# Who forms the low halves of the weights: GpSimd and VectorE, or VectorE alone

## The chip, the cores and the metric

The kernel runs on one core of one Trainium2 chip. The metric is the device time of one execution in microseconds (us).

## The reference

Four layers work on 256 context tokens and 256 latent tokens of 1024 channels. Layers 0 and 3 mix by a gated linear recurrence (HGRN2, 8 heads of 128), layer 1 by attention over a window and the context (16 heads of 64), layer 2 by a state-space scan (S5). Behind every mixer comes a feed-forward network (FFN) with a three-tap convolution. The part that matters here is the dense products:

```python
def conv_ffn(h, w_in, conv_w, conv_b, w_out):
    u = dwconv_centred(h @ w_in, conv_w, conv_b)
    a, v = jnp.split(u, 2, axis=-1)
    return (jax.nn.silu(a) * v) @ w_out

def hgrn2_mixer(h_ctx, h_lat, w_in, lower, out_g, w_out):
    ...
        q, i, g, zf, zb = jnp.split(h @ w_in, 5, axis=-1)
    ...
            f = lb + (1.0 - lb) * jax.nn.sigmoid(p[gate_idx])
            ...
            o, s = gla_chunk_scan(flip(p[0]), flip(1.0 - f), flip(p[1]), flip(logf), s0)
```

All inputs are float32. The last layer's output for the latent tokens is returned.

## The kernel before

Each dense product is made of three matmuls with operands of a shorter format (fp32r): activations and weights are each split into a high half (the value rounded to the short format) and a low half (the rest), and TensorE sums high by high, high by low, and low by high (`mm3`, L691 to L693; `vproj`, L727 to L729).

The weights come as a stream of 248 tiles of [128, up to 2048] float32 (class `Stream`). `_load` (L96) issues one DMA on SP's queue into `wraw` (two buffers). `_split` (L103) takes the next tile and puts a list of small jobs into `todo`: the two high halves `whi` on ScalarE (L112), the low halves `wlo = wraw - whi` (L115), and the load of the tile two further on. `step` (L128) emits one job of the list. `mm3` and `vproj` call it after every second k, that is after every six matmuls, so that the split of the next tile is spread over the products with the present one: eight steps for two projections of eight k. What is left over is emitted when the next tile is fetched (`get`, L141), or in a burst in a layer's `chain` (L511). No scheduler moves instructions: each engine runs its own in the order in which the program emits them.

The low half is formed in two parts, side by side: GpSimd (POOL in the profile) takes the first `share` of the columns, VectorE (DVE) the rest. `SH` (L68) holds the shares: 0.5, and 0.65 in the HGRN layers. `run` and `chain` set the share (L1829, L498, L554); the FFN of layer 3 runs with the HGRN share too, since the last `chain` ahead of it sets that one.

In an HGRN layer, while TensorE makes the projections of head h+1, a generator `attn` (L1054) works on head h, one round at each `tick` (L700): TensorE's small products of the block (L1106), then VectorE multiplies `FB` by the gates (`double`, L1077 and L1082), multiplies the gates `P` by each other (L1088) and copies the block into `S` (L1111). The next round's products need the new `FB`. The gate of the projection just made is applied on VectorE between the rounds (`gate`, L1047).

At the end of a stage `chain` (L495) makes the norm: a reciprocal on VectorE (L465), then the update of `x` and the next input `h`, with some of the elementwise work on GpSimd (L520, L581). TensorE has little else to do meanwhile. While layers 0 and 1 run their FFN, constants of the S5 layer are made (`s5_prep`, L1462: `W` on VectorE, L1483 to L1488, `Wt` on GpSimd, L1482).

Of the kernel before, what the change touches and what calls it, by code (L numbers as in the profile page):

```python
# [6 lines left out]
F32 = mybir.dt.float32  # L7
# [57 lines left out]
NN = 18  # L65
PC = 18
PN = 12
SH = (0.5, 0.5, 0.65, 0.5, 0.5)  # L68
RNG = ((0, 256), (256, 512))
EPS = 1e-6  # L70
MUL, ADD, SUB, MAX = ALU.mult, ALU.add, ALU.subtract, ALU.max
# [10 lines left out]
class Stream:  # L82
    def __init__(self, kern, bufs, lead, hl_bufs):
        self.k = kern
        self.plan = []
        self.bufs, self.lead, self.hl = bufs, lead, hl_bufs
        self.nl = self.ns = self.nu = 0
        self.raw, self.split = {}, {}
        self.share = SH[0]
        self.todo = []  # L90
        self.cap = 1 << 20

# [10 lines left out]
    def _split(self):  # L103
        k, nc = self.k, self.k.nc
        key, ap, n = self.plan[self.ns]
        r = self.raw.pop(self.ns)
        hi = k.wp.tile([128, 2048], F32R, name="whi", bufs=self.hl)
        lo = k.wp.tile([128, 2048], F32R, name="wlo", bufs=self.hl)
        m = int(n * self.share) // 64 * 64

        def high(a, b):
            nc.scalar.activation(hi[:, a:b], r[:, a:b], AF.Copy)  # L112

        def low(e, a, b):
            e.tensor_tensor(lo[:, a:b], r[:, a:b], hi[:, a:b].bitcast(F32), op=SUB)  # L115

        if m:
            self.todo += [(high, 0, m), (low, nc.gpsimd, 0, m)]
        if m < n:
            self.todo += [(high, m, n), (low, nc.vector, m, n)]  # L120
        if m and m < n:
            self.todo[-3:-1] = self.todo[-2:-4:-1]
        if self.nl < min(len(self.plan), self.cap):
            self.todo.append((self._load,))
        self.split[self.ns] = (hi, lo)
        self.ns += 1
# [28 lines left out]
class Kern:  # L155
# [32 lines left out]
        h = self.xp.tile([128, 2, 2, NK, 256], F32R, name="h")  # L188
        self.hh, self.hl = h[:, 0], h[:, 1]

# [1 line left out]
    def tick(self):  # L192
        if not self.gens:
            self.bgtick()
        if not self.draining:
            for g in list(self.soft):
                self.advance(g, self.soft)
        gens = list(self.gens)
        if self.pace and len(gens) > 1:
            self.turn += 1  # L200
            if self.turn % self.pace:
                gens = [gens[(self.turn - 1) % len(gens)]]
        for g in gens:
            self.advance(g, self.gens)
# [45 lines left out]
            except StopIteration:  # L250
                self.bg = None

# [1 line left out]
    def consts(self):  # L254
        nc, cp = self.nc, self.cp
        self.cc = cp.tile([128, 16], F32, name="cc")
        nc.sync.dma_start(self.cc, self.a["cc"])
        self.x = self.xp.tile([128, NK, T], F32, name="x")
        for k in range(NK):
            (nc.scalar if k % 2 else nc.sync).dma_start(self.x[:, k], self.a["xin"][:, k])  # L260
        self.sel = cp.tile([128, 2], F32, name="sel")
        nc.sync.dma_start(self.sel, self.a["sel"])
        self.ident = cp.tile([128, 128], F32, name="ident")
        nc.sync.dma_start(self.ident, self.a["ident"])
        self.vec = cp.tile([128, NVEC], F32, name="vec")
        nc.sync.dma_start(self.vec, self.a["vec"])
        self.y = self.xp.tile([128, 2, NK, 256], F32, name="y")
        self.new_h()
        self.ones = cp.tile([128, 1], F32, name="ones")
        nc.vector.memset(self.ones, 1.0)  # L270
        self.epsc = cp.tile([128, 1], F32, name="epsc")
        nc.vector.memset(self.epsc, EPS)
        self.mT = cp.tile([128, 4, 6, NK, 2], F32, name="mT")
        self.g1 = cp.tile([128, 4, 4, NK, 2], F32, name="g1")
        self.sT = cp.tile([128, NK, 32], F32, name="sT")
        nc.vector.memset(self.sT, 0.0)
        nc.scalar.activation(self.sT[:, :, 0:2], self.cc.rearrange("p (k i) -> p k i", i=2), AF.Silu)

# [1 line left out]
    def mod_setup(self, pool, bufs, first, n):  # L280
        self.mod_pool, self.MB = pool, bufs
        self.mod_nl = self.mod_nd = first
        self.mod_end = n
        self.mod_raw = {}
        self.mod_pend = None
        self.mod_order = [(0, s, b) for b in range(4) for s in (1, 0)]
        self.mod_order += [(l, s, b) for l in range(4) for s in (1, 0, 2, 4, 3, 5) for b in range(4) if l or s > 1]
        for i in range(bufs):
            if first == 0 and i == 2:
                self.ws.start()  # L290
            self.mod_load()
# [124 lines left out]
        if self.mod_pend is not None and self.mod_pend[0] <= idx:  # L416
            self.mod_flush()

# [1 line left out]
    def rstd_col(self, sqs, nb, n):  # L420
        nc = self.nc
        ps = self.aux()
        for b in range(nb):
            for i, q in enumerate(sqs):
                nc.tensor.matmul(ps[:, b:b + 1], q[:, b * 128:(b + 1) * 128], self.ones, start=(b == 0 and i == 0),
                                 stop=(b == nb - 1 and i == len(sqs) - 1), skip_group_check=True)
        r = self.np_.tile([128, 8], F32, name="rs", bufs=4)
        nc.scalar.activation(r[:, :nb], ps[:, :nb], AF.Sqrt, scale=1.0 / n, bias=self.epsc)
        nc.vector.reciprocal(r[:, 4:4 + nb], r[:, :nb])
        return r  # L430
# [64 lines left out]
    def chain(self, l, n, half, nxt):  # L495
        nc = self.nc
        a, b = RNG[half]
        self.ws.share = SH[1]  # L498
        if n is not None:
            for _ in range(CW[0] if half else C0 if n == 1 else CS[2] if nxt is not None and KINDS[nxt[0]] == 2 else C3):  # L500
                yield
# [49 lines left out]
            return  # L551
        yield
        _, bc = yield from self.rstd_sb(("x", half))
        self.ws.share = SH[self.shi]  # L554
        l2, n2 = nxt
        s0 = 0 if n2 == 0 else 3
        s5 = n2 == 0 and KINDS[l2] == 2
# [2 lines left out]
        for k in range(NK):  # L560
            g = self.g1[:, l2, n2, k, half:half + 1]
            m = self.mT[:, l2, s0, k, half:half + 1]
# [12 lines left out]
            else:  # L575
                hi, lo = self.hh[:, half, k], self.hl[:, half, k]
# [97 lines left out]
            while ws.todo:  # L674
                ws.step()

# [1 line left out]
    def H(self, k, half):  # L678
        if half is None:
            return self.hh[:, :, k, :], self.hl[:, :, k, :]  # L680
        return self.hh[:, half, k, :], self.hl[:, half, k, :]
# [158 lines left out]
            self.nc.scalar.activation(y, ps, AF.Copy)  # L840
        return done

# [1 line left out]
    def plan_ffn(self, l, halves):  # L844
        tail = FTAIL if l < 3 and KINDS[l + 1] == 2 else 0
        add = self.ws.add
# [143 lines left out]
            while self.bg is not None:  # L990
                self.bgtick()

# [1 line left out]
    def lower_prep(self):  # L994
        nc = self.nc
        lg = self.v("low").rearrange("p (l k) -> p l k", k=NK)
# [234 lines left out]
            if full:  # L1231
                self.finish(c0)

# [1 line left out]
    def plan_na(self, l):  # L1235
        for _ in self.plan_heads(l, ("qk",), (lambda j: self.a["b_qk"][j], lambda p: self.a["b_v"][p]), 1):
            self.plan_wo(l, 0, 2)
        for _ in range(2):
            self.plan_wo(l, 1, 2)
            self.plan_wo(l, 2, 2)  # L1240
# [128 lines left out]
                    c0 = c  # L1369
            self.finish(c0)  # L1370

# [1 line left out]
    def cmul(self, e, outr, outi, ar, ai, br, bi, t):  # L1373
        e.tensor_tensor(outr, ar, br, op=MUL)
        e.tensor_tensor(t, ai, bi, op=MUL)
        e.tensor_tensor(outr, outr, t, op=SUB)
        e.tensor_tensor(outi, ar, bi, op=MUL)
        e.tensor_tensor(t, ai, br, op=MUL)
        e.tensor_tensor(outi, outi, t, op=ADD)
# [436 lines left out]
    def run(self):  # L1816
        nc, tc = self.nc, self.tc
        for l in range(4):
            (self.plan_hgrn, self.plan_na, self.plan_s5, lambda l: None)[KINDS[l]](l)
            self.plan_ffn(l, (1,) if l == 3 else (0, 1))  # L1820
        self.consts()
        with tc.tile_pool(name="start", bufs=1) as sp:
            self.mod_setup(sp, 7, 0, 8)
            self.begin()
        self.mod_setup(self.wp, 1, 8, 96)
        for l in range(4):
            halves = (1,) if l == 3 else (0, 1)
            self.shi = (2, 3, 0)[KINDS[l]] if KINDS[l] < 3 else 0
            self.ws.share = SH[self.shi]  # L1829
            if KINDS[l] == 3:  # L1830
                self.drain()
                self.mod_until(l, 3)
                for half in halves:
                    for k in range(NK):
                        hi, lo = self.H(k, half)
                        y = self.y[:, half, k]
                        nc.vector.tensor_tensor(y, hi.bitcast(F32), lo.bitcast(F32), op=ADD)
                        self.sq_add(("y", half), k, y)
                    self.gens.append(self.chain(l, 1, half, (l, 2)))
                    self.drain()  # L1840
            else:
                (self.hgrn, self.na, self.s5)[KINDS[l]](l)
            if l == 3:
                self.drain()
            self.shi = 0 if l < 3 else 4
            self.ffn(l, halves, (l + 1, 0) if l < 3 else None)
        self.drain()
# [85 lines left out]
```

## Time and profile before

| | |
|---|---|
| time, median of 3 runs (lowest to highest) | 2995.45 us (2994.34 to 2996.59) |
| the profiled execution: its span, the only time listed for it | 3001.2 us |
| TensorE (PE) busy | 2769.3 us, 92% |
| VectorE (DVE) busy | 2016.9 us, 67% |
| ScalarE (ACT) busy | 1285.0 us, 43% |
| GpSimd (POOL) busy | 824.1 us, 27% |
| L115 on GpSimd, 248 instructions | 627.8 us, mean 2532 ns |
| L115 on VectorE, 248 instructions | 400.5 us, mean 1615 ns |
| granted TensorE clock, mean | 0.960 |

Busy times overlap between engines. Only work or waiting on the engine that is late adds to the time. PE is TensorE's matmul row. An idle time in front of an instruction is put down to the semaphore that came last. A granted clock of 1.00 is 2.4 GHz, 0.50 is 1.2 GHz.

### The profile page before, as it was taken

The numbers are of one execution on the slowest core, as the hardware profiler recorded it, in microseconds if no ns is written. First come the engines' busy times: TensorE is split into PE (matmuls) and PEld (weight loads), VectorE is DVE, ScalarE is ACT, GpSimd is POOL, SyncE is SP. The second block draws the span as 40 slices with busy tenths as digits, with TensorE's granted clock in tenths as the row PEclk, the third lists the DMA queues.
The fourth block names the chain that finished last, engine by engine and source line by source line (L and its number), as shares of the span: only waits on it lengthen the run. The fifth ranks groups of instructions, "written<-read, shape, count | busy, mean of one in ns | idle before, by whom it ended". The sixth has DMA issues, their size and how long they took to land.

```text
span 3001.2 us, 53651 instructions
## 1 busy us (share of the span) xinstructions
PE 2769.3 (92%) x21814; PEld 2283.6 (76%) x21814; DVE 2016.9 (67%) x3979; ACT 1285.0 (43%) x2154; POOL 824.1 (27%) x440
## 2 busy tenths in 40 slices
PE   8999997999999999889999876989999888998998
PEld 5777776877788777777778734878888887776998
DVE  5676767776657555687555675378677777776776
ACT  4333333633344544553333565453333453332644
POOL 1111112243324111234332311332221342222443
PEclk9999998999999999999999988999999989998998
DMA  6222321255424342235553388323433442232543
GB/s 248 91 100 85 114 86 71 94 186 187 160 105 144 113 162 106 102 128 192 198 197 140 129 238 255 139 87 139 147 133 138 153 171 102 99 113 89 186 173 116
DMA packets 127046, 421.28 MB, mean 140 GB/s; under 512 B 36048, under 2 KB 55760, under 8 KB 102096
## 3 DMA queue, kind: packets, MB, share of 16 engines
q1 hardware_dynamic: 118608, 391.64, 37.5%
q0 software_dynamic: 5472, 23.07, 2.2%
q8 instruction: 172, 2.82, 0.4%
q10 hardware_dynamic: 2720, 3.15, 0.3%
q14 instruction: 74, 0.61, 0.1%
HBM read 392.78 MB, written 29.23 MB: 141 GB/s over the span
## 4 chain that ended last, share of the span: by engine, by line
PE 65%; DVE 20%; ACT 6%; issue 4%; DMA 3%; SPq 1%; POOL 1%; DVEq 0%; ACTq 0%; POOLq 0%
PE acc L691 16%; PE acc L692 15%; PE acc L693 15%; DVE wlo L115 3%; ACT whi L112 2%; PE aux L317 2%; PE aux L1106 2%; DVE FB L1077 2%; PE acc L727 1%; PE acc L729 1%; PE acc L728 1%; DVE y L564 1%; DVE u L896 1%; DVE P L1047 1%; PE aux L1146 1%
## 5 line engine op out<-in xcount | busy, mean ns | idle before, releaser
L115 POOL TENSOR_TENSOR wlo<-wraw,whi 128x1024 fp32r<-128x1024 f32 (+5 forms) x248 | 627.8, 2532 | 1738.2 <-ACT whi L112 1634.2
L691 PE MATMUL acc<-h,whi 128*128 128x512 f32 (+1 forms) x2368 | 869.7, 367 | 26.8 <-ACT h L577 15.7
L692 PE MATMUL acc<-h,whi 128*128 128x512 f32 (+1 forms) x2368 | 843.2, 356 | 21.1 <-DVE h L584 16.7
L693 PE MATMUL acc<-h,wlo 128*128 128x512 f32 (+1 forms) x2368 | 838.8, 354 | 6.1 <-POOL wlo L115 4.0
L691 PEld LDWEIGHTS acc<-h,whi 128*128 128x128 f32 x2368 | 459.1, 194 | 96.5 <-ACT h L577 18.8
L115 DVE TENSOR_TENSOR wlo<-wraw,whi 128x1024 fp32r<-128x1024 f32 (+5 forms) x248 | 400.5, 1615 | 184.5 <-ACT whi L112 154.5
L692 PEld LDWEIGHTS acc<-h,whi 128*128 128x128 f32 x2368 | 459.7, 194 | 81.4 <-DVE h L584 24.0
L693 PEld LDWEIGHTS acc<-h,wlo 128*128 128x128 f32 x2368 | 459.6, 194 | 67.0 <-POOL wlo L115 4.6
L112 ACT ACTIVATE whi<-wraw 128x1024 fp32r<-128x1024 f32 (+5 forms) x496 | 479.5, 1014 | 68.5 <-PE acc L692 51.2
L691 PE MATMUL acc<-gh,whi 128*128 128x256 f32 (+1 forms) x872 | 297.7, 341 | 11.2 <-ACT gh L897 11.2
L693 PE MATMUL acc<-gh,wlo 128*128 128x256 f32 (+1 forms) x872 | 289.6, 332 | 3.0 <-POOL wlo L115 3.0
L692 PE MATMUL acc<-gl,whi 128*128 128x256 f32 (+1 forms) x872 | 289.7, 332 | 1.0 <-DVE gl L898 0.7
L886 ACT ACTIVATE u<-acc,vec 128x512 f32<-128x512 f32 (+1 forms) x190 | 127.4, 691 | 215.1 <-PE acc L693 214.6
L1077 DVE TENSOR_TENSOR FB<-FB,P 128x256 f32<-128x256 f32 x384 | 165.4, 473 | 37.9 <-PE aux L1106 35.2
L691 PEld LDWEIGHTS acc<-gh,whi 128*128 128x128 f32 x872 | 167.5, 192 | 28.8 <-ACT gh L897 12.0
L889 DVE SCALAR_TENSOR_TENSOR u<-acc,vec,u 128x510 f32<-128x510 f32 (+1 forms) x190 | 122.0, 642 | 97.6 <-ACT u L886 97.5
L693 PEld LDWEIGHTS acc<-gh,wlo 128*128 128x128 f32 x872 | 167.0, 192 | 19.9 <-POOL wlo L115 3.8
L692 PEld LDWEIGHTS acc<-gl,whi 128*128 128x128 f32 x872 | 167.2, 192 | 17.7 <-DVE gl L898 2.3
L896 DVE TENSOR_TENSOR u<-u,u 128x512 f32<-128x512 f32 (+1 forms) x95 | 107.5, 1131 | 37.5 <-ACT u L895 34.2
L897 ACT ACTIVATE gh<-u 128x512 fp32r<-128x512 f32 (+1 forms) x95 | 52.3, 551 | 179.6 <-DVE u L896 179.6
L890 DVE SCALAR_TENSOR_TENSOR u<-acc,vec,u 128x510 f32<-128x510 f32 (+1 forms) x190 | 123.1, 648 | 6.7
L1106 PEld LDWEIGHTS aux<-FB 128*32 128x32 f32 (+1 forms) x4416 | 58.4, 114 | 82.0 <-DVE FB L1077 37.4
(299 smaller groups left out, 4328.4 us busy)
## 6 DMA issues: line engine op xcount, KB each, us to landing
wm<-in_w_mod SPq DMA_DIRECT2D x192, 512.0 KB, 5.0
wraw<-in_f_w_in SPq DMA_DIRECT2D x89, 1024.0 KB, 4.8
wraw<-in_fo SPq DMA_DIRECT2D x44, 896.0 KB, 4.5
wraw<-in_a_qz SPq DMA_DIRECT2D x18, 1024.0 KB, 4.9
wraw<-in_a_zg SPq DMA_DIRECT2D x18, 1024.0 KB, 4.9
wraw<-in_fo SPq DMA_DIRECT2D x16, 1024.0 KB, 4.9
wraw<-in_a_v SPq DMA_DIRECT2D x15, 1024.0 KB, 4.9
wraw<-in_c_glu SPq DMA_DIRECT2D x12, 1024.0 KB, 4.8
```

Source lines behind the costliest of these rows:

```text
L112: nc.scalar.activation(hi[:, a:b], r[:, a:b], AF.Copy)
L115: e.tensor_tensor(lo[:, a:b], r[:, a:b], hi[:, a:b].bitcast(F32), op=SUB)
L317: nc.tensor.matmul(ps[32 * j:32 * j + 32, :256], self.sT[:, k, :], r[q][:, j, :], start=(q == 0), stop=(q == 1), tile_position=(0, 32 * j))
L691: nc.tensor.matmul(ps, wh[:, k], hh, start=(first and k == 0), stop=False, **kw)
L692: nc.tensor.matmul(ps, wh[:, k], hl, start=False, stop=False, **kw)
L693: nc.tensor.matmul(ps, wl[:, k], hh, start=False, stop=(last and k == nk - 1), **kw)
L886: nc.scalar.activation(u, ps[c], AF.Identity, scale=w(1), bias=self.vec[:, cb0 + ch:cb0 + ch + 1])
L889: nc.vector.scalar_tensor_tensor(u3[:, :, 1:], p3[:, :, :255], w(0), u3[:, :, 1:], op0=MUL, op1=ADD)
L890: nc.vector.scalar_tensor_tensor(u3[:, :, :255], p3[:, :, 1:], w(2), u3[:, :, :255], op0=MUL, op1=ADD)
L896: nc.vector.tensor_tensor(us[1], us[0], us[1], op=MUL)
L1077: nc.vector.tensor_tensor(o, o, p, op=MUL)
L1106: nc.tensor.matmul(o, FB[:, d, 1 - d, c:c + w], r, start=True, stop=True, tile_position=(0, w * q))
```

## The change

GpSimd forms no low half any more. VectorE forms all of it, in `parts` pieces per tile: two, and four where the share was 0.65 (`LP`). ScalarE's high half is cut at half of the columns everywhere. The jobs of a tile are now: two highs, two or four lows, one load.

```diff
-SH = (0.5, 0.5, 0.65, 0.5, 0.5)
+LP = (2, 2, 4, 2, 2)
...
-        m = int(n * self.share) // 64 * 64
+        m = n // 128 * 64
...
-        def low(e, a, b):
-            e.tensor_tensor(lo[:, a:b], r[:, a:b], hi[:, a:b].bitcast(F32), op=SUB)
-
-        if m:
-            self.todo += [(high, 0, m), (low, nc.gpsimd, 0, m)]
-        if m < n:
-            self.todo += [(high, m, n), (low, nc.vector, m, n)]
-        if m and m < n:
-            self.todo[-3:-1] = self.todo[-2:-4:-1]
+        def low(a, b):
+            nc.vector.tensor_tensor(lo[:, a:b], r[:, a:b], hi[:, a:b].bitcast(F32), op=SUB)
+
+        cuts = [round(n * i / self.parts / 64) * 64 for i in range(self.parts)] + [n]
+        self.todo += [(high, 0, m), (high, m, n)]
+        self.todo += [(low, a, b) for a, b in zip(cuts, cuts[1:])]
         if self.nl < min(len(self.plan), self.cap):
             self.todo.append((self._load,))
...
-        self.ws.share = SH[1]
+        self.ws.parts = LP[1]
```

`SH[...]` becomes `LP[...]` in the other two places as well. In the order of the program GpSimd's 248 subtractions are gone and VectorE's go from 248 to 674: 232 of 1024 columns, 298 of 512, 72 of 896, and 72 smaller ones. Lines behind L115 stand three lower in the changed program.

VectorE's order at the start of the rounds of a head of layer 3, while the next head is projected, before (`FB`, `P`, `S` belong to the rounds; `sg` and `ol` close the head before):

```order
L115 TENSOR_TENSOR wlo<-wraw,whi 128x768
L1162 TENSOR_TENSOR sg<-sg,aux 128x256
L1167 TENSOR_TENSOR ol<-sg,oh 128x256
L390 TENSOR_TENSOR mT<-aux,vec 128x4
L398 SCALAR_TENSOR_TENSOR g_98<-mT,vec 128x4
L1077 TENSOR_TENSOR FB<-FB,P 128x2x128 x2
L1082 TENSOR_TENSOR FB<-FB,P 128x2x128
L1088 TENSOR_TENSOR P<-P 128x512
L1111 COPY_PREDICATED S<-masks,aux 128x256
L1077 TENSOR_TENSOR FB<-FB,P 128x2x64x2 x2
```

The same place with the change:

```order
L115 TENSOR_TENSOR wlo<-wraw,whi 128x512 x2
L1159 TENSOR_TENSOR sg<-sg,aux 128x256
L1164 TENSOR_TENSOR ol<-sg,oh 128x256
L387 TENSOR_TENSOR mT<-aux,vec 128x4
L395 SCALAR_TENSOR_TENSOR g_98<-mT,vec 128x4
L115 TENSOR_TENSOR wlo<-wraw,whi 128x512
L1074 TENSOR_TENSOR FB<-FB,P 128x2x128 x2
L1079 TENSOR_TENSOR FB<-FB,P 128x2x128
L1085 TENSOR_TENSOR P<-P 128x512
L1108 COPY_PREDICATED S<-masks,aux 128x256
L115 TENSOR_TENSOR wlo<-wraw,whi 128x512
L1074 TENSOR_TENSOR FB<-FB,P 128x2x64x2 x2
```

The one piece of 768 columns has become four of 512: two stand where it stood, one in front of the first round and one in front of the second. The pieces of the next tile follow in the same way among the last rounds.

VectorE's order in the norm behind the mixer of layer 1, at the reciprocal of the second norm, before:

```order
L584 SCALAR_TENSOR_TENSOR h<-y,mT,h 128x256 x3
L115 TENSOR_TENSOR wlo<-wraw,whi 128x1024
L465 RECIPROCAL bc_12117<-aux 128x256
L523 SCALAR_TENSOR_TENSOR y<-y,g_98,bc_12117 128x256
L529 TENSOR_TENSOR x<-x,y 128x256
```

The same place with the change:

```order
L581 SCALAR_TENSOR_TENSOR h<-y,mT,h 128x256 x3
L115 TENSOR_TENSOR wlo<-wraw,whi 128x1024 x2
L462 RECIPROCAL bc_12173<-aux 128x256
L520 SCALAR_TENSOR_TENSOR y<-y,g_98,bc_12173 128x256
L526 TENSOR_TENSOR x<-x,y 128x256
```

The reciprocal now stands behind both halves of the low weights instead of behind one.

## Rows read from the trace of the kernel before

**Rows 1.** The page: busy time of the engines, whole span.

```profile
PE 2769.3 (92%) x21814; PEld 2283.6 (76%) x21814; DVE 2016.9 (67%) x3979; ACT 1285.0 (43%) x2154; POOL 824.1 (27%) x440
```

**Rows 2.** By stage: us, PE, PEld, DVE, ACT, POOL busy (xcount), PEclk, DMA, GB/s.

```profile
75.00:450.00 375.00, 355.10 (x4325) 280.16 (x4324) 253.72 (x588) 124.34 (x203) 64.27 (x22) 0.98 0.27 95
...
2784.00:2959.00 175.00, 172.87 (x1454) 169.62 (x1453) 134.30 (x169) 95.17 (x155) 87.00 (x30) 1.00 0.51 183
2003.00:2337.00 334.00, 332.56 (x1579) 276.95 (x1578) 256.27 (x432) 123.24 (x173) 72.17 (x32) 1.00 0.38 133
```

**Rows 3.** TensorE's waits, 75 to 450 us (heads of layer 0): us, times, longest.

```profile
PE aux L1106 <- DVE FB L1077: 10.6, 8, 1.7
...
PE aux L1120 <- DVE FB L1077: 2.8, 3, 1.3
```

**Rows 4.** TensorE's waits, 2445 to 2745 us (heads of layer 3).

```profile
PE aux L1106 <- DVE FB L1077: 10.2, 7, 1.5
PE aux L1106 <- DVE FB L1082: 4.7, 3, 2.3
...
PE aux L1120 <- DVE FB L1077: 2.2, 2, 1.1
```

**Rows 5.** Timeline of one head of layer 3, VectorE and then GpSimd.

```profile
2548.57 3.03 DVE L1047 TENSOR_SCALAR P<-P,lb 128x512 f32<-128x512 f32 x1
...
2558.42 0.55 DVE L1047 TENSOR_SCALAR P<-P,lb 128x512 f32<-128x512 f32 x1
...
2548.40 2.92 POOL L115 TENSOR_TENSOR wlo<-wraw,whi 128x1280 fp32r<-128x1280 f32 x1 [9.73 <-ACT whi L112]
```

**Rows 6.** Timeline of TensorE in the head before that one.

```profile
2515.14 0.65 PE L1106 MATMUL aux<-FB 128*32 128x32 f32 x16 [1.53 <-DVE FB L1077]
```

**Rows 7.** As rows 2, slow stretches in layer 3's heads, first and last.

```profile
2517.10:2520.50 3.40, 3.40 (x16) 2.42 (x15) 3.04 (x10) 0.00 (x0) 0.00 (x0) 0.50 0.00 0
2728.70:2732.10 3.40, 3.40 (x48) 3.14 (x45) 2.81 (x8) 0.00 (x0) 0.00 (x0) 0.50 0.02 5
```

**Rows 8.** VectorE's groups by shape, whole run: busy us, mean ns, idle before.

```profile
L115 DVE TENSOR_TENSOR wlo<-wraw,whi 128x1024 fp32r<-128x1024 f32 x116 | 203.9, 1758 | 104.8 <-ACT whi L112 91.3 <-issue 13.5
...
L896 DVE TENSOR_TENSOR u<-u,u 128x256 f32<-128x256 f32 x36 | 48.4, 1346 | 9.9 <-ACT u L895 7.7
```

**Rows 9.** Timeline of VectorE, instructions beside which GpSimd was idle.

```profile
599.32 0.69 DVE L898 TENSOR_TENSOR gl<-u,gh 128x512 fp32r<-128x512 f32 x1 [0.70 <-ACT gh L897]
...
599.93 1.22 DVE L115 TENSOR_TENSOR wlo<-wraw,whi 128x1024 fp32r<-128x1024 f32 x1
...
2867.48 0.95 DVE L115 TENSOR_TENSOR wlo<-wraw,whi 128x768 fp32r<-128x768 f32 x1
```

**Rows 10.** VectorE's groups by shape, 2445 to 2745 us.

```profile
L1077 DVE TENSOR_TENSOR FB<-FB,P 128x256 f32<-128x256 f32 x128 | 50.3, 434 | 5.3 <-PE aux L1106 5.3
L115 DVE TENSOR_TENSOR wlo<-wraw,whi 128x768 fp32r<-128x768 f32 x23 | 38.3, 1664 | 11.1 <-ACT whi L112 9.1 <-issue 2.0
...
L1047 DVE TENSOR_SCALAR P<-P,lb 128x512 f32<-128x512 f32 x12 | 21.1, 1755 | 0.1
```

**Rows 11.** Timeline of one norm behind layer 1: ScalarE, GpSimd, VectorE.

```profile
1283.30 1.99 ACT L112 ACTIVATE whi<-wraw 128x1024 fp32r<-128x1024 f32 x2
...
1284.48 2.40 POOL L115 TENSOR_TENSOR wlo<-wraw,whi 128x1024 fp32r<-128x1024 f32 x1 [1.91 <-ACT whi L112]
...
1285.38 2.58 DVE L115 TENSOR_TENSOR wlo<-wraw,whi 128x1024 fp32r<-128x1024 f32 x1 [1.34 <-issue]
```

**Rows 12.** The chain that ended last: a low half right before a reciprocal, first and last.

```profile
527.84 3.04 DVE wlo L115
...
2390.86 2.54 DVE wlo L115
```

**Rows 13.** TensorE's waits, whole run.

```profile
PE acc L693 <- POOL wlo L115: 10.4, 10, 1.9
...
PE aux L1541 <- DVE W L1488: 3.4, 3, 1.2
```

More of the change, by code (lines that the diff above doesn't have):

```diff
@@ L88, in __init__ @@
         self.raw, self.split = {}, {}
-        self.share = SH[0]
+        self.parts = LP[0]
         self.todo = []
@@ L553, in chain @@
         _, bc = yield from self.rstd_sb(("x", half))
-        self.ws.share = SH[self.shi]
+        self.ws.parts = LP[self.shi]
         l2, n2 = nxt
@@ L1828, in run @@
             self.shi = (2, 3, 0)[KINDS[l]] if KINDS[l] < 3 else 0
-            self.ws.share = SH[self.shi]
+            self.ws.parts = LP[self.shi]
             if KINDS[l] == 3:
```

## Prediction

> **What bounds the kernel.** First the page's busy times: TensorE works 92% of the span, VectorE 67%, GpSimd 27% [rows 1]. So the time is TensorE's stream of matmuls plus the places where that stream stops, and the change adds no matmul and removes none. Then the busy times by stage: the FFN of layer 2 has TensorE at 332.56 of 334 us and that of layer 3 at 172.87 of 175 [rows 2]. There nothing is to be won, and VectorE, with 256.27 and 134.30 us, has room. In the heads of layer 0 TensorE is idle for 20 of 375 us. What it waits for there and in the heads of layer 3, the list of its waits tells: above all VectorE's work on `FB` in the rounds, 10.6 + 2.8 us [rows 3] and 10.2 + 4.7 + 2.2 us [rows 4], 30.5 us together.
>
> Why VectorE is late there, the timeline of a head shows: the gate L1047 takes 3.03 us, and the same instruction ten microseconds later 0.55 us [rows 5]. The difference, 2.48 us, lies under a low half on GpSimd that runs from 2548.40 for 2.92 us: VectorE's instruction starts 0.17 us after GpSimd's and ends just after it. While GpSimd reads its two operands, a VectorE instruction that comes to it stands still. The group rows say that this is common: the 1024-column low half on VectorE has a mean of 1758 ns [rows 8] and takes 1.22 us where GpSimd is idle [rows 9]; the product L896 has a mean of 1346 ns for 256 columns [rows 8], where a product of that size has a mean of 434 ns [rows 10].
>
> **VectorE's total.** Prices without GpSimd beside it: 0.69 us for 512 columns, 0.95 for 768, 1.22 for 1024 [rows 9]; by interpolation about 1.08 for 896. The 674 pieces cost 232 x 1.22 + 298 x 0.69 + 72 x 1.08 + about 72 x 0.6 = 610 us, an estimate from these rows. The 248 of before cost 400.5 us, so 210 us are added. Taken away is what GpSimd's subtractions cost VectorE's other instructions: L896 alone 36 x (1.35 - 0.43) = 33 us, L1047 in layer 3's heads 12 x (1.76 - 0.55) = 14.5 us [rows 8, 10], and many smaller groups. VectorE's busy time should therefore rise by 60 to 160 us, to some 2080 to 2180 us, 70 to 72% of the span. GpSimd falls by 627.8 us to about 200. What counts is where it falls.
>
> **Heads of layers 0 and 3.** In the head of layer 3, 2.48 us of standing still gave TensorE a wait of 1.53 us in the head before [rows 6], so about 0.95 us of delay is absorbed. With the change no instruction stands still for that long: one piece of 0.69 us stands in front of a round, and in the worst case two rounds in a row have one, 1.38 us, 0.43 more than is absorbed. Two such places in a head and 14 heads with rounds leave 12 us of waits. Of 30.5 us, 18 us go. Bounds: all of it, 30 us, where the pieces fall into VectorE's idle time; and below nothing, in the third rival. One thing comes on top: behind the 1.53 us wait the granted clock is 0.50 for 3.4 us [rows 7], that is 1.2 GHz in place of 2.4, while TensorE is busy for all of it; that is 1.7 us of work lost. There are six such stretches of 3.4 us in the heads of layer 3, the first and the last shown, 10 us in all. A shorter wait may still be followed by one, so none of it is in the sum; it is the lower end.
>
> VectorE's own sum in those heads is nearly even: 23 tiles cost 38.3 us and would cost 23 x 4 x 0.69 = 63.5, 25 us more, against 14.5 us of L1047 and smaller groups that are no longer blocked [rows 10].
>
> Here a rule of the Trainium skill speaks against the change. "Perfetto Trace Analysis", section Optimizing Scalar/DVE Operations, says that with VectorE saturated some of its work may be better off on GpSimd, and that grouping into larger operations then raises the throughput; four pieces on VectorE are the opposite of both. It adds that the two engines share a read port and that such a move might not help. By its first half the stages in which VectorE is the late engine would get slower, the third rival; the trace agrees with its last half, with 2.48 us of VectorE's time lost under 2.92 us of GpSimd's.
>
> **Norms.** In eight places of the chain a low half stands right in front of the reciprocal of a norm [rows 12]. In one of them the two highs begin at 1283.30 and take 1.99 us; GpSimd's low starts behind the first at 1284.48; VectorE's, behind the second at 1285.38, has to wait for GpSimd and ends at 1287.96 [rows 11]. With the change the first piece starts at about 1284.4 and the second ends by 1284.4 + 2 x 1.22 = 1286.9, a microsecond sooner. Eight of these are 8 us; I take half, 4 us, since part of the norms run beside matmuls. Ends: 0 and 8.
>
> **Waits for GpSimd's low itself.** TensorE waits 10.4 us for it, in ten places [rows 13]. Two pieces of VectorE take 2.44 us, as GpSimd's one does, but the first is there after half of that. I take 4 us; ends 0 and 10.
>
> **Preparation of the S5 layer.** TensorE waits 3.4 us in three places for `W` [rows 13], a product of VectorE behind one of GpSimd. GpSimd's queue becomes free for `Wt`. I take 3 us; ends 0 and 4.
>
> **What it costs.** A tile in two pieces has 1.22 us more of VectorE. In the FFNs TensorE covers that: in layer 2, some 32 tiles add 39 us to 256 of 334; in layer 3, some 30 tiles of four pieces add 30 x (2.76 - 0.95) = 54 us to 134 of 175, and 33 us of L896's stall go [rows 2, 8]. Were that cover gone, layer 3's FFN would have VectorE at 188 us against TensorE's 173, 13 us over the present 175. In the norms and the first products behind them an extra piece can stand in front of an `h` that TensorE needs: I take 6 us for some 20 passes at 0.3 us; ends 0 and 24 (one piece in each). A load is issued two steps later in a tile of four pieces; it lies on SP's queue behind the last low, as before behind GpSimd's, and a tile ahead of its use. I cost that at nothing: in layer 2's FFN 334 us for some 32 tiles [rows 2] are 10 us per tile, with room for it, and in layer 3's FFN the load leaves when VectorE has done its last low, which is so today.
>
> **Sum.** -18 - 4 - 4 - 3 + 6 = -23 us. The profiled span, 3001.2 us, lies 5.75 us over the median of the runs, 0.2%, which is also about what a measurement of this kernel can tell from no change. I take the sum off the median: 2995.45 - 23 = 2972 us. With all terms at their good ends, the clock's 10 us too, it is 2995.45 - 62 = 2933, which asks for everything at once.
>
> **Rivals.**
> - *The clock comes back as well.* With the waits in layer 3's heads gone, the 10 us of slow clock go too, and the norms give their 8 in place of 4: 2972 - 14 = 2958 us. For it: the slow stretches of the heads stand behind the waits. Against: TensorE also pauses there for other reasons.
> - *The waits only move.* The rounds then wait for ScalarE's copies or for the next low piece, and what the heads gain is eaten by 1.22 us per tile elsewhere. The sum is -4 - 4 + 6, 2993 us. For it: VectorE's sum hardly falls anywhere.
> - *Rounds bound by VectorE, slower.* In the rounds VectorE has no idle time to speak of (5.3 us in front of 128 of L1077 [rows 10]). If GpSimd's blocks mostly fell into slack and the four pieces all stand on the path, a tile of a head costs 1.81 us more (4 x 0.69 - 0.95); 23 tiles in layer 3 and about 21 in layer 0 give 80 us at the most. It decides from where more than 18 us of that is on the path: that is what the heads are to give. At half of it: 40 us in place of -18, 2972 + 58 = 3030; at a third, 27 us, 3017.
>
> **Chances.** The forecast case, 2962 to 2986, has 0.5; the clock's case 0.25; the waits that only move 0.13; rounds bound by VectorE 0.12. The range goes from 2948 to 2993: it takes in the first case, most of the second and the edge of the third. Faster by over 0.2%, under 2989.5 us: 0.77. Within 0.2%: 0.11. Slower: 0.12.
>
> **What would show it.** Right: L1047 never over about 0.6 us; L115 on VectorE with 674 instructions and means of 0.69 and 1.22 us; GpSimd at about 200 us; TensorE's waits for `FB` in the heads down from 30 to some 12 us; fewer stretches at a clock of 0.50 around 2500 to 2700. Wrong: VectorE's instructions as long as before without GpSimd beside them; waits for `FB` as long or longer, with L115 in front; FFN of layer 3 longer than 175 us; or TensorE waiting for `wlo` from VectorE by more than the 10.4 us that it waits for GpSimd's today.

## The result, and the profile after

The change makes the kernel faster: 2920.8 us (median; 2918.75 to 2924.45) against 2996.02 us of the kernel before on the same chip, ratio 0.9744, 95% interval 0.9732 to 0.9756. That is 75 us less; the forecast was 23. The time lies below the range. The profiled execution has a span of 2918.4 us, 82.8 below that of before.

The page, busy times of the engines over the whole span:

```profile
PE 2740.2 (94%) x21814; PEld 2267.2 (78%) x21814; DVE 1992.1 (68%) x4405; ACT 1290.1 (44%) x2154; POOL 194.9 (7%) x192
```

Span and granted clock:

```profile
core 0: 2918.4 us, clock 0.969
```

Against [rows 1], the difference of 82.8 us splits into two parts. TensorE's idle time, span less busy, goes from 231.9 to 178.2 us: -53.7. And its busy time falls by 29.1 us though not a matmul is gone. That is the clock: at a mean of 0.960 the span loses 0.040 x 3001.2 = 120 us to it, at 0.969 it loses 90.

VectorE's busy time falls by 24.8 us, although its low halves went from 400.5 to 601.7 us. The groups by shape of the changed kernel, VectorE, whole run (busy us, mean ns, idle before):

```profile
L115 DVE TENSOR_TENSOR wlo<-wraw,whi 128x1024 fp32r<-128x1024 f32 x232 | 285.4, 1249 | 81.6 <-ACT whi L112 81.4
L115 DVE TENSOR_TENSOR wlo<-wraw,whi 128x512 fp32r<-128x512 f32 x298 | 195.6, 693 | 39.3 <-ACT whi L112 39.2
...
L893 DVE TENSOR_TENSOR u<-u,u 128x256 f32<-128x256 f32 x36 | 15.2, 423 | 7.5 <-ACT u L892 7.0
L1044 DVE TENSOR_SCALAR P<-P,lb 128x512 f32<-128x512 f32 x28 | 15.1, 540 | 1.0 <-ACT P L1043 1.0
```

The gate (L1047 before) has a mean of 0.54 us, where in layer 3's heads it had 1.76 [rows 10], the FFN's product 0.42 in place of 1.35 [rows 8]. All that is not L115 fell by 24.8 + 201.2 = 226 us.

Where in the program the time went can be cut exactly, since all 21,814 matmuls stand in the same order in both traces: the stretches below begin and end at the same matmuls. In order: up to the first heads, heads of layer 0, norm behind them, norm behind layer 2 with the start of layer 3, heads of layer 3, FFN of layer 3. Before (columns as in [rows 2]):

```profile
6.20:89.90 83.70, 77.01 (x502) 54.36 (x506) 43.41 (x94) 32.52 (x53) 12.95 (x5) 0.94 0.58 224
...
89.90:424.80 334.90, 319.85 (x4012) 251.62 (x4012) 237.53 (x546) 114.29 (x183) 61.33 (x21) 0.99 0.26 93
...
424.80:571.50 146.70, 122.04 (x1105) 104.06 (x1107) 107.22 (x231) 60.00 (x126) 33.63 (x25) 0.88 0.25 88
2333.80:2456.40 122.60, 104.28 (x702) 96.39 (x701) 90.95 (x126) 64.82 (x114) 52.86 (x32) 0.89 0.44 154
...
2456.40:2744.40 288.00, 263.72 (x3003) 222.32 (x3002) 208.69 (x431) 104.19 (x162) 68.80 (x24) 0.96 0.31 111
...
2801.30:2976.70 175.40, 169.99 (x1402) 166.22 (x1401) 128.74 (x165) 91.08 (x150) 83.23 (x29) 0.98 0.50 180
```

With the change:

```profile
5.90:83.90 78.00, 73.21 (x502) 51.14 (x506) 42.82 (x103) 32.54 (x53) 0.00 (x0) 1.00 0.61 231
...
83.90:401.00 317.10, 314.68 (x4014) 249.50 (x4016) 226.06 (x609) 114.36 (x183) 0.00 (x0) 1.00 0.29 99
...
401.00:542.50 141.50, 119.22 (x1101) 101.88 (x1100) 107.84 (x259) 60.54 (x126) 13.27 (x16) 0.90 0.28 94
2292.60:2403.50 110.90, 97.85 (x702) 90.67 (x700) 87.59 (x145) 64.82 (x114) 16.97 (x16) 0.94 0.49 169
...
2403.50:2670.30 266.80, 255.06 (x3002) 218.67 (x3001) 195.91 (x502) 104.41 (x162) 0.00 (x0) 0.98 0.35 119
...
2727.90:2893.90 166.00, 165.33 (x1403) 162.98 (x1402) 124.93 (x252) 93.19 (x150) 0.00 (x0) 1.00 0.54 190
```

The six give 5.7 + 17.8 + 5.2 + 11.7 + 21.2 + 9.4 = 71 of the 83 us. The other 12 lie between the third and the fourth of them, from layer 0's FFN to layer 2's (1762.3 us before, 1750.1 after). The heads are 39 of the 71: 25 us of idle time and 14 us of TensorE's busy time, which is the clock. VectorE has less to do in both (237.53 to 226.06, 208.69 to 195.91), though it makes 2048 columns of a tile where it made 768.

TensorE's waits for the rounds, in the heads of layer 0 (83.9 to 401 us) and then of layer 3 (2403.5 to 2670.3):

```profile
PE aux L1103 <- DVE FB L1074: 0.7, 1, 0.7
...
PE aux L1103 <- DVE FB L1079: 3.6, 8, 0.6
PE aux L1103 <- DVE FB L1074: 2.6, 4, 1.1
...
PE aux L1117 <- DVE FB L1074: 1.1, 1, 1.1
```

8.0 us where [rows 3, 4] have 30.5.

How GpSimd's subtraction acts on its neighbour is seen best at one place of the kernel before, the timeline of GpSimd and then of VectorE:

```profile
2475.46 3.35 POOL L115 TENSOR_TENSOR wlo<-wraw,whi 128x1280 fp32r<-128x1280 f32 x1 [5.26 <-ACT whi L112]
...
2475.94 0.44 DVE L1111 COPY_PREDICATED S<-masks,aux 128x256 f32<-128x256 uint32 x1
2476.27 2.69 DVE L1047 TENSOR_SCALAR P<-P,lb 128x256 f32<-128x256 f32 x1
2478.89 0.41 DVE L1077 TENSOR_TENSOR FB<-FB,P 128x256 f32<-128x256 f32 x1
```

The copy into S runs beside the subtraction in its usual 0.44 us. The next instruction, which has a mean of 0.41 us with the change, ends only when GpSimd does, and the round's product stands behind it. GpSimd starts here when `whi` is ready, in the middle of a round.

VectorE's own part of the low half stands still in the same way, and where it does, the split does not even shorten the work that is split. One such place, GpSimd and VectorE side by side in the kernel before, and then VectorE alone with a whole tile in one piece (run with one piece in the HGRN layers, below):

```profile
2461.81 2.96 POOL L115 TENSOR_TENSOR wlo<-wraw,whi 128x1280 fp32r<-128x1280 f32 x1 [3.30 <-ACT whi L112]
...
2462.55 3.03 DVE L115 TENSOR_TENSOR wlo<-wraw,whi 128x768 fp32r<-128x768 f32 x1 [1.53 <-ACT whi L112]
```

```profile
2479.65 2.28 DVE L115 TENSOR_TENSOR wlo<-wraw,whi 128x2048 fp32r<-128x2048 f32 x1
```

VectorE is held for 3.03 us by 768 columns here (the mean in layer 3's heads is 1.66 [rows 10]), and takes 2.28 us for all 2048 when GpSimd is idle.

### The profile page after: what moved, and what is told of

Same layout as the page of the kernel before. It is cut to its first block, busy times and chain, and to the rows that moved or that the text cites. A ratio compares the mean times of both kernels' runs of the same rounds, so it can differ in the third digit from the quotient of the medians.

```text
span 2918.4 us, 53174 instructions
## 1 busy us (share of the span) xinstructions
PE 2740.2 (94%) x21814; PEld 2267.2 (78%) x21814; DVE 1992.1 (68%) x4405; ACT 1290.1 (44%) x2154; POOL 194.9 (7%) x192
## 4 chain that ended last, share of the span: by engine, by line
PE 72%; DVE 16%; ACT 5%; DMA 3%; issue 2%; SPq 1%; POOL 0%; ACTq 0%; DVEq 0%; POOLq 0%
PE acc L688 19%; PE acc L689 18%; PE acc L690 17%; DVE wlo L115 3%; PE aux L314 2%; PE aux L1103 2%; PE acc L724 2%; PE acc L726 1%; PE acc L725 1%; DVE bc L462 1%; DVE y L561 1%; ACT whi L112 1%; PE aux L1143 1%; PE aux L383 1%; DVE y L520 1%
## 5 line engine op out<-in xcount | busy, mean ns | idle before, releaser
L688 PE MATMUL acc<-h,whi 128*128 128x512 f32 (+1 forms) x2368 | 868.3, 367 | 24.8 <-ACT h L574 15.3
L115 DVE TENSOR_TENSOR wlo<-wraw,whi 128x512 fp32r<-128x512 f32 (+5 forms) x674 | 601.7, 920 | 153.0 <-ACT whi L112 152.6
L112 ACT ACTIVATE whi<-wraw 128x1024 fp32r<-128x1024 f32 (+3 forms) x496 | 479.5, 1014 | 66.6 <-PE acc L689 51.7
L1074 DVE TENSOR_TENSOR FB<-FB,P 128x256 f32<-128x256 f32 x384 | 145.2, 421 | 31.9 <-PE aux L1103 29.3
L724 PE MATMUL acc<-whi,h 128*128 128x256 f32 x384 | 115.2, 300 | 2.2 <-ACT whi L112 1.2
L726 PE MATMUL acc<-wlo,h 128*128 128x256 f32 x384 | 110.0, 287 | 4.1 <-DVE wlo L115 4.1
L725 PE MATMUL acc<-whi,h 128*128 128x256 f32 x384 | 109.7, 286 | 0.0
```

The lines of the kernel that those rows point to most:

```text
L115: nc.vector.tensor_tensor(lo[:, a:b], r[:, a:b], hi[:, a:b].bitcast(F32), op=SUB)
L688: nc.tensor.matmul(ps, wh[:, k], hh, start=(first and k == 0), stop=False, **kw)
L724: nc.tensor.matmul(o, hh, wh[:, :, k, :], start=(k == 0), stop=False)
L725: nc.tensor.matmul(o, hl, wh[:, :, k, :], start=False, stop=False)
L726: nc.tensor.matmul(o, hh, wl[:, :, k, :], start=False, stop=(k == NK - 1))
L1074: nc.vector.tensor_tensor(o, o, p, op=MUL)
```

## Experiments

Theory A: GpSimd's two-operand reading stops VectorE, and that costs time wherever something waits for VectorE. Its rivals are that the sizes of the prediction hold (B), that what counts is the length of one stall (C), that it is the size of VectorE's pieces (D), and that GpSimd's low halves came late themselves (E). Each edit is shown as the lines that it adds to the changed kernel, in `_split` unless said. `V` and `G` are VectorE and GpSimd, `pieces` the change's list of lows, `half` half of the columns, `m` the columns that GpSimd had (0.5, or 0.65 where `parts` is 4). Each ratio is to the kernel before, run beside it on the same chip, with its 95% interval; differences to the change are differences of these gains.

### The change in the HGRN layers alone, and elsewhere alone

The second kernel has `!=` in place of `==`.

```diff
+        if self.parts == 4:
+            self.todo += [(high, 0, half), (high, half, n)] + pieces
+        else:
+            self.todo += [(high, 0, m), (high, m, n), (low, G, 0, m), (low, V, m, n)]
```

> VectorE alone (four pieces) in the tiles that had the share of 0.65, that is the HGRN layers and the FFN of layer 3; in all other tiles GpSimd forms half as before. Theory A (GpSimd's two-operand subtraction stops VectorE's instructions, and that costs time wherever a round or a norm stands behind them; the HGRN heads have most such places): some 50 of the 75 us, a time of 2940 to 2952 us, GpSimd busy about 450 us. Rival B, the sizes of the prediction (the heads give 18 us, the clock 10 more): 2966 to 2978 us, and the other layers hold the rest.

> The reverse: VectorE alone in two pieces where the share was 0.5, GpSimd 0.65 of the columns in the HGRN layers and the FFN of layer 3 as before. Theory A: some 25 us less than before, 2966 to 2976 us; the two parts add up to the whole gain of 75 us within 6. Rival B: 2940 to 2952 us. If the two gains do not add up, the parts act on each other.

Measured: 2946.1 us, ratio 0.9826 (0.9814 to 0.9839), 51.2 us less; and 2971.05 us, ratio 0.9911 (0.9898 to 0.9924), 26.3 us less (before: 2997.34). Together 77.5, the change as a whole 75.2: the parts add up. They also add up by stage: between the matmuls that bound them above, the heads of layers 0 and 3 take 317.0 and 266.0 us in the first run, as with the change, and 334.8 and 287.9 us in the second, as before. B falls.

### Shorter pieces on GpSimd too

```diff
+        g, v = m // 128 * 64, m + (n - m) // 128 * 64
+        self.todo += [(high, 0, m), (high, m, n), (low, G, 0, g), (low, V, m, v), (low, G, g, m), (low, V, v, n)]
```

> The kernel before with its shares, but GpSimd's part and VectorE's part each cut into two pieces, so GpSimd reads as many columns as before and no subtraction of it is longer than 1.5 us. Theory A (what counts is how many columns GpSimd reads beside VectorE): 2980 to 3000 us, and VectorE's busy time stays near 2000 us. Rival C (what counts is that one stall of 2.5 us is longer than the 0.95 us that the rounds absorb, and shorter stalls are absorbed): under 2965 us, most of the gain.

Measured: 2986.47 us, ratio 0.996 (0.9947 to 0.9972). Eleven of the 75 us, and none of it in the heads: they take 334.7 and 288.0 us, as before. So C falls, as far as pieces of this length tell: GpSimd's largest, of 640 columns, take 1.67 us on average, a little over the 1.5 expected, in place of 2.95, and that is still more than the 0.95 us of the prediction. TensorE's largest wait for VectorE over the whole run, in the kernel before and here:

```profile
PE aux L1106 <- DVE FB L1077: 25.4, 22, 1.7
...
PE aux L1105 <- DVE FB L1076: 24.3, 22, 1.7
```

### The subtraction back on GpSimd, for nothing

```diff
+        def dummy(a, b):
+            s = k.wp.tile([128, 640], F32, name="scr", bufs=1)
+            for c in range(a, b, 640):
+                d = min(c + 640, b)
+                G.tensor_tensor(s[:, :d - c], r[:, c:d], hi[:, c:d].bitcast(F32), op=SUB)
...
+        self.todo += [(high, 0, half), (last,)] + pieces
```

`last` makes the second high half and then calls `dummy(0, m)`.

> The changed kernel, and beside it GpSimd makes the same subtraction over the same columns as in the kernel before (0.5 and 0.65 of each tile, in pieces of at most 640 columns) into a scratch tile that nothing reads. Only the next load into wraw and the next high half wait for it. Theory A (GpSimd's reads stop VectorE): at least what the kernel before takes, 2985 to 3050 us, with VectorE's busy time over 2250 us. Rival E (what cost time before was that GpSimd's low halves came late themselves): 2915 to 2935 us.

Measured: 3083.08 us, ratio 1.0275 (1.025 to 1.03), more than expected. The result goes nowhere, and costs 162 us against the change. E falls. That the dummy holds `wraw` and `whi` longer explains little of it: ScalarE is idle for 4.1 us until GpSimd is done with a buffer, and for 20.8 us until a load into `wraw` has landed, 9.7 with the change. The page, and a group of VectorE:

```profile
PE 2797.0 (91%) x21814; PEld 2292.7 (74%) x21814; DVE 2348.4 (76%) x4405; ACT 1287.7 (42%) x2154; POOL 1042.3 (34%) x683
...
L1056 DVE TENSOR_SCALAR P<-P,lb 128x512 f32<-128x512 f32 x28 | 29.7, 1064 | 0.1
```

VectorE runs the same 4405 instructions as with the change and is busy for 356 us more, for 847 us more on GpSimd: 0.42 us per microsecond. The gate has doubled again.

### One operand, and none

The dummy as `G.tensor_copy(s[:, :d - c], r[:, c:d])`:

> The same with a copy of wraw by GpSimd, one operand read in place of two, into the scratch tile. Theory A1 (only an instruction of GpSimd with two operands stops VectorE): 2915 to 2935 us, and VectorE's busy time within 30 us of 1992. Theory A2 (any reading by GpSimd stops VectorE): 2960 to 3050 us.

Measured: 2946.11 us, ratio 0.9828 (0.9812 to 0.9845), 25 us over the change, between A1 and A2. GpSimd is busy for 379 us more, VectorE for 83 us (2075.5), 0.22 per microsecond. Reading one operand stops VectorE too; a piece of 640 columns, 0.87 us, does it for a shorter time than the subtraction's 1.90. Timeline of GpSimd, then of VectorE:

```profile
74.38 1.85 POOL L125 COPY scr<-wraw 128x640 f32<-128x640 f32 x2 [6.18 <-DMA wraw<-in_a_v]
...
74.40 2.37 DVE L113 TENSOR_TENSOR wlo<-wraw,whi 128x512 fp32r<-128x512 f32 x2 [3.04 <-ACT whi L110]
```

Two pieces, 2 x 0.69 alone [rows 9], take 2.37 us.

The kernel before, with GpSimd writing zeros where it subtracted:

```diff
+            G.memset(lo[:, a:b].bitcast(F32), 0.0)
...
+        self.todo += [(high, 0, m), (high, m, n), (zero, 0, m), (low, V, m, n)]
```

> The shares of the kernel before, but GpSimd writes zeros where it formed its part of the low half, and reads nothing; VectorE forms its own part in one piece as before. So 0.5 and 0.65 of the low halves are left out. It is the kernel before without GpSimd's reading, and the changed kernel without the 210 us of pieces that VectorE takes over. Theory A: 2900 to 2921 us, VectorE busy near 1680 us; the distance to 2921 is the price of the added pieces, which the prediction put at 6 us and the heads' 12 us of waits that stay. If writes by GpSimd stop VectorE as well: 2960 to 2995 us.

Measured: 2887.74 us, ratio 0.963 (0.9612 to 0.9648), VectorE busy 1701.2 us: 109 us under before, 33 under the change, and 12 under the range of theory A. ScalarE's high halves are cut as before here, and as with the change in the dummy runs, so the other cut is not what gains. Two places, GpSimd and VectorE in each, and the free price of the second instruction from the changed kernel's groups (2394 to 2672 us) in a fence of its own:

```profile
2337.96 0.95 POOL L122 MEMSET wlo<- 128x1024 f32 x1 [0.92 <-POOL wlo L122]
...
2338.15 0.96 DVE L113 TENSOR_TENSOR wlo<-wraw,whi 128x768 fp32r<-128x768 f32 x1 [1.14 <-issue]
...
2445.99 1.17 POOL L122 MEMSET wlo<- 128x1280 f32 x1 [9.91 <-PE acc L695]
...
2446.00 1.43 DVE L1053 TENSOR_SCALAR P<-P 128x512 f32<-128x512 f32 x1 [0.70 <-ACT FB L1052]
```

```profile
L1048 DVE TENSOR_SCALAR P<-P 128x512 f32<-128x512 f32 x12 | 5.1, 422 | 0.0
```

A subtraction of VectorE beside GpSimd's writing takes 0.96 us, as alone (0.95, [rows 9]). The one-operand L1053 stands still beside it: 1.43 us in place of 0.42.

The Trainium skill says the first of the two in "SBUF — State Buffer", section Who interferes with whom: a VectorE instruction with two inputs in SBUF contends with a GpSimd instruction that reads, "not with one that only writes it", and whichever comes second stands until the other has ended. The subtraction beside the zeros agrees, with 0.96 us; so does VectorE's low half at 2462.55 us of the kernel before, which starts 0.74 us behind GpSimd's and takes 3.03 us.

### How many pieces

`LP = (2, 2, 2, 2, 2)`, `(1, 1, 1, 1, 1)` and `(2, 2, 1, 2, 2)`:

> The change with two pieces per tile everywhere, HGRN layers too. Theory A: the pieces' size matters little, 2915 to 2930 us. Rival D (the small pieces are what keeps the rounds from waiting: 1.22 us in front of each of two rounds is 1.5 us more than the 0.95 us absorbed): 2935 to 2960 us, with TensorE's waits for FB in layer 3's heads back at 15 us or more.

> The changed kernel with one piece per tile: VectorE forms 2048 columns in one instruction of some 2.3 us, 248 instead of 674 instructions. Theory D of the prediction (a round absorbs 0.95 us and no more, so a block of 2.3 us in front of a round stops TensorE by some 1.4 us, 7 to 14 times in each of the two HGRN layers, and in the norms the reciprocal comes later still): 2940 to 2965 us, with TensorE's waits for FB back at 20 us or more. If it is the total of VectorE's work that counts: 2912 to 2925 us, since some 45 us of starts of instructions go.

> The changed kernel with one piece per tile in the HGRN layers (and the FFN of layer 3) and two elsewhere. With one piece everywhere the waits for FB did not come back (13.0 us against 12.1). If the heads take a block of 2.3 us in their stride: 2920 to 2935 us, FB waits of 10 to 15 us, and most of the 49 us of the run with one piece came from the norms of all layers and the waits for wlo. If the heads do not: 2940 to 2960 us.

Measured: 2923.48 us, ratio 0.975 (0.9737 to 0.9763), no difference from four pieces; 2969.93 us, 0.9898 (0.9884 to 0.9911), 45 us over the change and a little over the range of D; 2930.73 us, 0.9779 (0.9762 to 0.9796), 7 us over it. TensorE's waits with one piece everywhere:

```profile
PE acc L690 <- DVE wlo L115: 18.1, 17, 2.7
PE aux L446 <- ACT sl L484: 18.0, 11, 4.6
...
PE aux L1117 <- DVE FB L1074: 6.5, 10, 1.1
PE aux L1103 <- DVE FB L1074: 6.5, 9, 1.3
...
PE aux L1103 <- DVE FB L1079: 3.4, 5, 1.4
```

One piece costs in the norms (`sl`, their squares: 8.9 with the change) and in `wlo` itself (6.3); these two rows are 21 of the 45 us, and what the rest is was not taken apart. The third expectation's 13.0 against 12.1 counted the first rows only: with all its rows for `FB` the run with one piece waits 18.9 us in 28 places, the change 14.0 in 25, before 37.3 in 34. So blocks of 2.3 us of VectorE's own give back 5 of the 23 us. In the one head that I followed in the trace with one piece in the HGRN layers, they stand at 2470.34 and 2479.65 us, where the program has put them, behind the last round of a head and in front of the first of the next; GpSimd's, above, comes between two rounds. That this holds for all heads was not tried. D holds outside the HGRN layers and layer 3's FFN, where 38 of the 45 us lie, and for a fifth of the heads' waits.

### GpSimd's other work

`HP` and `TP` emptied and L476 on VectorE: 101 instructions of the norms move to VectorE (and 33 of ScalarE's that made operands for GpSimd go), in the changed kernel and, alone, in the kernel before; then the products `Wt` too (`v, g = nc.vector, nc.vector` in `s5_prep`).

> The changed kernel with the elementwise work of the norms that is left on GpSimd (101 instructions, 89 us) moved to VectorE too. Theory A says that these stop VectorE as well while they run, so that the move costs little: 2915 to 2928 us. Rival F (in the norms VectorE is the engine that everything waits for, and GpSimd's help is worth more there than what it blocks): 2930 to 2950 us.

> The kernel before, with GpSimd's elementwise work in the norms moved to VectorE and nothing else. If what blocks is GpSimd's work in general, the move gains here as well, about the 21 us that it gained in the changed kernel: 2970 to 2985 us. If GpSimd's low halves beside the norms block VectorE there anyway, the move gains less: 2985 to 3000 us.

> The changed kernel with the norms' elementwise work and the products Wt of the S5 preparation on VectorE too, so that GpSimd computes almost nothing. The 64 products take VectorE some 44 us; GpSimd's stop VectorE for 13.5 us today, and W waits for them. They lie beside the FFNs of layers 0 and 1, where TensorE covers VectorE. Theory A with cover: 2893 to 2901 us, no different from 2900. If the cover is too small: 2902 to 2915 us.

Measured: 2899.66 us, ratio 0.9669 (0.9652 to 0.9687); 2977.51 us, 0.9924 (0.9908 to 0.9941); 2903.09 us, 0.9672 (0.9659 to 0.9685). The move gains 21.6 us over the change (96.8 less 75.2) and 21.5 without it: the two do not depend on each other, and the first of these kernels beats the change. I had expected no gain. The page shows why the move costs VectorE nothing:

```profile
PE 2731.9 (94%) x21814; PEld 2256.3 (78%) x21814; DVE 1987.6 (69%) x4506; ACT 1283.3 (44%) x2121; POOL 105.9 (4%) x91
```

VectorE has 101 instructions more and is busy for 4.5 us less: 89 us on GpSimd had held it for about what the work costs VectorE itself. How much of the 21.6 us comes from that, and how much from ScalarE's 33 instructions or from norms that no longer pass through GpSimd, was not separated. By its time the last run lies just over the range for enough cover; by the ratios `Wt` changes nothing beyond the interval: VectorE is busy for 26 us more, and TensorE covers it, as the FFNs of layers 0 and 1 let one expect.

## Why the prediction was wrong in size

- **Mechanism: right.** GpSimd's reading makes VectorE stand still, and waits for `FB` come from that. It is shown by the dummy subtraction (+162 us with nothing waiting for its result) and by the zeros (-109 us).
- **Waits of the heads: nearly right.** Forecast: 12 of 30.5 us stay. Measured: 8.0; TensorE's idle time there falls by 25 us, against 18 in the sum. The reason for what stays was weak. The 0.95 us "absorbed" is a stall of one head less a wait of another, and blocks of 2.3 us, far over it, give back only 5 us.
- **Clock left out of the sum: wrong.** The rival had 10 us in layer 3's heads, from six slow stretches; a seventh starts at 2489.7 us, ahead of the one that [rows 7] call the first. Between the same matmuls TensorE's busy time falls by 8.7 us there and 5.2 in layer 0, over the whole run by 29.1. This term alone is larger than the forecast.
- **"There nothing is to be won" in layer 3's FFN: wrong.** The stretch was read from 2784 to 2959 us, where TensorE works 172.87 of 175. Between the matmuls above it has 5.4 us of idle time and a clock of 0.98, and gives 9.4 us. In layer 2's FFN nothing was won, as forecast: 334.0 us from the same matmul to the same matmul with the change too.
- **Norms -4, `wlo` -4, S5 preparation -3, cost +6: the step that failed most.** These stand for all that is outside the heads, -5 us; by the profiles it is -44, 28.5 of idle time and 15 of TensorE's busy time. Counted was a microsecond on the low half itself, and that came: the place of [rows 11] takes 3.44 us now from the first high to the last low, 4.66 before. Put at nothing outside the heads was what the sum had for the heads alone, that VectorE's other instructions are stopped as well; the clock was at nothing everywhere. Layer 3's start alone gives 11.7 us, the first products of layer 0 another 5.7, and VectorE alone outside the HGRN tiles gives 26 us by itself. Which instructions there give how much was not taken apart. The waits that had a term of their own are a small part: TensorE's for `wlo` fell from 17.9 us (10.4 of them for GpSimd's part, [rows 13]) to 10.4, those for `W` from 6.5 (the 3.4 of [rows 13] and the row below) to 3.1, a fall of 3.4 us where 3 was forecast. That row of the kernel before, and then the timeline of the norm with the change, ScalarE and VectorE:

```profile
PE aux L1513 <- DVE W L1486: 3.1, 1, 3.1
```

```profile
1249.72 1.99 ACT L112 ACTIVATE whi<-wraw 128x1024 fp32r<-128x1024 f32 x2
...
1250.80 2.36 DVE L115 TENSOR_TENSOR wlo<-wraw,whi 128x1024 fp32r<-128x1024 f32 x2 [0.34 <-ACT whi L112]
```

- **VectorE's total: wrong in sign.** Forecast: 60 to 160 us more. The pieces were right (601.7 against an estimate of 610), the relief was not: I took L896's 33 and L1047's 14.5 us and "many smaller groups"; it was 226 us.
- **Cost of the added pieces: too low.** The forecast had 6 us and the 12 us of waits that stay. The zeros' run says about 33 us. That is no exact price: its zeros are there earlier than a low half would be, and they still stop one-operand instructions of VectorE. Gain and cost were both too small, the gain by far more: 109 against 29.
- **Rivals.** Bound by VectorE: refuted, VectorE's load falls in the heads. Waits only move: refuted. The clock's rival was the nearest, 37 us short.
- **The rule weighed against the change.** "Perfetto Trace Analysis", section Optimizing Scalar/DVE Operations, of the Trainium skill advises to offload and to group where VectorE is saturated. VectorE is busy for 67% of the span here and 72% of layer 3's heads, so this condition does not hold, and the rule should not have weighed against the change: offloading cost 75 us, grouping into one piece 45. Its last half, that a move between these two engines might not help, is what the traces bear out.

## What to carry to other kernels

Work given to GpSimd is not free because GpSimd has time: compare the mean of VectorE's groups beside it and without it over all shapes, and take the whole difference, not only that of the place where TensorE's wait is longest. Then cut both traces at the same matmuls; what a stage can give is its idle time plus what its granted clock takes. If GpSimd must work beside a loaded VectorE, the runs of this case say what did least harm: zeros written and nothing read, then one operand read, then two.

## Not expected of the hardware

- Waits and slow clock do not go in step. With one piece in the HGRN layers TensorE is idle for 2925.7 - 2732.5 = 193.2 us, 15 more than with the change, but the mean clock is 0.974 instead of 0.969. The mean over the span alone says little, since it goes from 0.966 to 0.974 over the four executions of that one kernel. But layer 3's heads show it too, in this run and in the one with one piece everywhere:

```profile
2401.10:2673.20 272.10, 254.64 (x3002) 215.89 (x3001) 191.89 (x431) 104.18 (x161) 0.00 (x0) 0.99 0.33 117
...
2445.80:2717.90 272.10, 254.74 (x3003) 216.03 (x3002) 191.74 (x431) 104.17 (x161) 0.00 (x0) 0.99 0.34 117
```

  They have 17.5 and 17.4 us of idle time at 0.99; the change has 11.7 at 0.98. Which pause is followed by a slow stretch stays open.
- GpSimd's zeros, which read nothing, stop a one-operand instruction of VectorE (1.43 against 0.42 us) and leave a two-operand one alone.
- It goes the other way as well. Where VectorE comes first, GpSimd stands: in the run with the dummy subtraction a piece of 640 columns that starts 0.05 us behind a subtraction of VectorE takes 2.60 us, against a mean of 1.90:

```profile
701.97 2.60 POOL L125 TENSOR_TENSOR scr<-wraw,whi 128x640 f32<-128x640 f32 x1 [3.00 <-ACT whi L110]
...
701.92 3.73 DVE L113 TENSOR_TENSOR wlo<-wraw,whi 128x1024 fp32r<-128x1024 f32 x2 [0.89 <-ACT whi L110]
```
